# A hybrid decoder block: attention's filling dealt anew with its rows three ahead, and the scan's transposes of y two steps later

## The chip, the cores and the metric

The kernel runs on one core of one Trainium2 chip. The metric is the device time of one launch in microseconds (us). The kernel before takes 2052.62 us, the median of three runs from 2051.77 to 2053.46.

Engine names are those of the profile: PE is the matmul engine (PEld its weight loads), DVE VectorE, ACT ScalarE, POOL GpSimd, SP the engine that issues most DMAs.

## The reference

One layer of a parallel-branch block over 1024 tokens of width 1024, float32:

```python
h = rms_norm(x, norm_w)
proj = h @ w_in
z, xbc, dt_raw, pool_u, pool_gate, qkv, sb_gate, merge = split(proj)
y_ssm  = mamba2_branch(z, xbc, dt_raw, ...) @ w_proj_ssm   # chunked scan, 8 chunks of 128, 32 heads of 64
y_pool = pool_branch(pool_u, pool_gate, ...) @ w_proj_pool
y_sb   = stick_breaking_branch(qkv, sb_gate) @ w_proj_sb   # 16 heads of 64
merged = sum of sigmoid(merge gate) * branch over the three
out = rms_norm(x + merged @ w_out, final_norm_w)

# attention, for a block of 128 queries and all keys before them
z = q k^T * scale
log_beta = log_sigmoid(z); log_one_minus = where(causal, log_sigmoid(-z), 0)
later = reversed exclusive cumsum(log_one_minus)
att = where(causal, exp(log_beta + later), 0);  o = att v

# scan, for a chunk and a head
y = (C B^T * decay) (dt x) + exp(a_cum) C prev_state + d_skip x
state = state * exp(sum a) + B^T (decay_states dt x)
y_ssm_in = rms_norm(y * silu(z)) * ssm_norm_w              # norm over all 2048 channels
```

## The kernel before, in words

A projection product is kept near float32 by splitting both operands in a high and a low part and adding three products, hi x hi, hi x lo, lo x hi (`gemm_b` at L396 with 512 columns, `gemm_a` at L405 with 256). A block of 256 projection columns is 96 such 512-wide matmuls, or 192 of 256 columns. Weights come by DMA as raw halves; ACT rounds the high part (L128) and DVE subtracts it (L129).

The work runs in five parts: norm and convolution inputs, attention, the scan, pooling, and the merge. In attention and in the scan the branch's own work leaves gaps on PE, and blocks of projections that are wanted later are dealt into them as *filling*: a queue of generators, one matmul at a step, from which `fill(ns)` takes as many as a budget in ns allows. A 512-wide matmul counts 216 ns there, a 256-wide one 109. `ensure(name)` runs the queue on until a block is finished.

**Attention** (`attention_part`) goes by units: pair p of heads (8), head hd in the pair (2), and pair ip of query blocks (4, the innermost), 64 units in all. Unit ip holds two *rows*, query blocks 2ip and 2ip+1, whose lengths are 256 ip + 128 and 256 ip + 256 keys.

- `stage_qk` makes one row: PE multiplies q by k into a PSUM tile z (pool of three, L892, L893, L895 for the mask), ACT takes two sigmoids (om L896, be L899), DVE sweeps om with a running product from the right (L901) and multiplies it into be (L902). om has two tiles, be four.
- `stage_tr` transposes a 256 x 256 piece of a unit's two rows on PE (L919) into one of two PSUM tiles; ACT rounds it (L921) and DVE subtracts the rounded part (L922).
- `stage_av` multiplies by v on PE (L945) into one PSUM tile, which ACT copies out at the end of every second unit (L950).

Unit m emits its transposes and, three behind, the products; between these pieces it makes both rows of unit m+1 and deals its share of the filling. The filling belongs to windows of about eight units: blocks ("vz", p+1) and ("qk", p+1) are v, z, q and k of the next pair, and two windows get other blocks of z (`ATT_FILL`). The share of a unit is its weight over the sum of the weights of its window; weights rise with ip from 0.64 to 1.36. PE keeps the order of the code in attention; the other engines are ordered by a scheduler.

**The scan** (`ssd_part`) has 32 steps of (chunk c, head group hg), with PE, DVE, POOL and ACT all in the order of the code. In step m of the loop: loads by SP; `stage_e(m+2)` makes the decay matrix E on ACT (L1149, L1150) and multiplies it with a masked matrix on POOL (L1151); `stage_a(m+1)` transposes x on PE (L1158) and scales it on DVE (L1160 to L1164); `stage_y(m-1)` multiplies y by the gate z on DVE (yz, L1204) and sums squares on ACT (L1205); `finish` makes the root of a whole chunk; `scale(m-5)` multiplies yz by that root on DVE (L1215); half a share of filling; `stage_b(m)` makes y and the state (PE L1174 to L1180, DVE L1183 to L1192, POOL L1186); another half share; `stage_c(m-5)` transposes the scaled yz on PE (ytr, L1221), ACT copies it with a weight (L1224), and SP stores it (L1225). A chunk's four yz lie in one tile, and there are two such tiles. The loop has 32 + 5 turns.

## Time and profile before

| | us |
|---|---|
| median of three runs | 2052.62 |
| profiled execution | 2052.7 |
| its span, first to last instruction | 2050.9 |
| PE busy | 2002.7 (98%) |
| DVE busy | 1392.3 (68%) |
| ACT busy | 955.6 (47%) |
| POOL busy | 301.0 (15%) |

Busy time is a union of an engine's instructions, so PE at 98% has 48 us in which it ran none. The busy time of an operation that two engines contend for includes the time it is held. In the rows, a name left of the arrow is what is written, names right of it what is read.

### The profile page before, as it was taken

The page shows a single profiled execution, that of the slowest core. Times are in us where ns is not written, and L with a number is a line of the kernel's source. Part 1 is how long each engine was busy: PE and PEld are TensorE (multiplying, and loading weights), DVE is VectorE, ACT ScalarE, POOL GpSimd, SP SyncE. Part 2 cuts the span into 40 slices and gives each one's busy share as a digit, 9 for nine tenths or more (in the row PEclk, how much of TensorE's full clock was granted, in tenths as well). Part 3 has the DMA queues.
Part 4 walks back from the last instruction along what each step waited for, and adds up shares of the span by engine and source line. Part 5 has one row for each costly group of instructions (what it writes and reads, how often), then busy time and mean ns, then how long its engine had stood idle before and what let it go on. Part 6 is the DMA issues. An engine that isn't in the chain of part 4 may idle for free.

```text
span 2050.9 us, 28716 instructions
## 1 busy us (share of the span) xinstructions
PE 2002.7 (98%) x10880; PEld 1687.6 (82%) x10880; DVE 1392.3 (68%) x1891; ACT 955.6 (47%) x1936; POOL 301.0 (15%) x412
## 2 busy tenths in 40 slices
PE   8999999999999999999999999999999999999998
PEld 6978888888898898898888987777788788888887
DVE  6786777768377888877788847998857724425434
ACT  4353333323256666656566557666643413313221
POOL 3000000000002211211112114453300002221000
PEclk9999999999999999999999999999999999999999
DMA  5323323233511121121211246665464625443422
GB/s 202 95 97 103 124 82 123 94 113 103 177 46 47 43 68 37 42 75 50 57 38 51 73 160 195 206 204 179 152 210 136 224 92 176 140 137 104 153 73 82
DMA packets 116153, 233.95 MB, mean 114 GB/s; under 512 B 9776, under 2 KB 59696, under 8 KB 116016
## 3 DMA queue, kind: packets, MB, share of 16 engines
q1 hardware_dynamic: 115728, 231.92, 35.2%
q8 instruction: 86, 1.41, 0.3%
q14 instruction: 51, 0.42, 0.1%
q10 hardware_dynamic: 288, 0.20, 0.0%
HBM read 168.38 MB, written 63.70 MB: 113 GB/s over the span
## 4 chain that ended last, share of the span: by engine, by line
PE 66%; DVE 22%; ACT 6%; issue 4%; DMA 1%; DVEq 0%; POOL 0%; SPq 0%; ACTq 0%; POOLq 0%
PE mm L396 17%; PE mmx L396 15%; PE mm L405 10%; PE mmx L299 9%; DVE om L901 4%; PE mmx L405 3%; DVE acc L358 3%; PE av L945 2%; PE mm L299 2%; DVE be L902 2%; PE tr L919 2%; DVE yz L1215 1%; DVE attT L922 1%; DVE w L129 1%; PE yd L1174 1%
## 5 line engine op out<-in xcount | busy, mean ns | idle before, releaser
L396 PE MATMUL mm<-hT,w 128*128 128x512 f32 x1656 | 443.2, 408 | 2.9 <-DVE hT L592 2.8
L396 PEld LDWEIGHTS mm<-hT,w 128*128 128x128 f32 x1656 | 299.3, 189 | 71.7 <-issue 15.3
L405 PE MATMUL mm<-w,hT 128*128 128x256 f32 x2112 | 292.6, 286 | 0.1
L405 PEld LDWEIGHTS mm<-w,hT 128*128 128x128 f32 x2112 | 265.2, 190 | 0.8 <-ACT qb L836 0.5
L396 PE MATMUL mmx<-x,w 128*128 128x512 f32 x1008 | 230.3, 389 | 0.0
L396 PEld LDWEIGHTS mmx<-x,w 128*128 128x128 f32 x1008 | 189.2, 188 | 39.3
L901 DVE TENSOR_TENSOR_SCAN om<-om,zero 128x128 f32<-128x128 f32 (+7 forms) x128 | 181.9, 1422 | 31.9 <-ACT om L896 30.9
L129 DVE TENSOR_TENSOR w<-raw,w 128x1024 fp32r<-128x1024 f32 x104 | 134.0, 1291 | 91.8 <-ACT w L128 91.5
L921 ACT CAST attT<-tr 128x512 fp32r<-128x512 f32 (+2 forms) x224 | 98.7, 441 | 139.4 <-DVE attT L922 89.2
L128 ACT CAST w<-raw 128x1024 fp32r<-128x1024 f32 x104 | 109.1, 1051 | 58.3 <-PE mmx L396 27.7
L922 DVE TENSOR_TENSOR attT<-tr,attT 128x512 fp32r<-128x512 f32 (+2 forms) x224 | 110.4, 495 | 36.7 <-ACT attT L921 35.4
L396 PE MATMUL mm<-x,w 128*128 128x512 f32 x528 | 122.6, 389 | 0.0
L1304 ACT ACTIVATE gt<-gt 128x1024 f32<-128x1024 f32 x32 | 34.0, 1062 | 180.7 <-DMA gt<-d_gate 172.7
L396 PEld LDWEIGHTS mm<-x,w 128*128 128x128 f32 x528 | 99.1, 188 | 20.6
L896 ACT ACTIVATE om<-z 128x128 f32<-128x128 f32 (+2 forms) x192 | 94.2, 502 | 34.9 <-PE z L895 32.9
L902 DVE TENSOR_TENSOR be<-be,om 128x128 f32<-128x128 f32 (+7 forms) x128 | 101.3, 792 | 11.5
L396 PE MATMUL mmx<-hT,w 128*128 128x512 f32 x456 | 105.0, 390 | 0.0
L919 PE MATMUL tr<-cm,be 128*128 128x128 f32 x576 | 91.7, 275 | 8.9 <-DVE attT L922 6.7
L396 PEld LDWEIGHTS mmx<-hT,w 128*128 128x128 f32 x456 | 85.4, 188 | 17.6
L1151 POOL TENSOR_TENSOR E<-E,cbm 128x1024 f32<-128x1024 f32 x32 | 78.5, 2452 | 145.3 <-issue 70.2
L899 ACT ACTIVATE be<-z 128x128 f32<-128x128 f32 (+2 forms) x192 | 93.8, 506 | 0.1
L299 PE MATMUL mmx<-tt,w 128*128 128x512 f32 x360 | 88.5, 397 | 0.3
(258 smaller groups left out, 3507.0 us busy)
## 6 DMA issues: line engine op xcount, KB each, us to landing
raw<-in_wblk SPq DMA_DIRECT2D x148, 512.0 KB, 3.8
E<-d_act SPq DMA_DIRECT2D x32, 512.0 KB, 4.1
gt<-d_gate SPq DMA_DIRECT2D x32, 512.0 KB, 3.8
d_gate<-cx SPq DMA_DIRECT2D x20, 512.0 KB, 5.0
xi<-d_x SPq DMA_DIRECT2D x32, 256.0 KB, 3.1
zs<-d_z SPq DMA_DIRECT2D x32, 256.0 KB, 4.1
d_ssm<-yt SPq DMA_DIRECT2D x32, 256.0 KB, 3.1
xraw<-d_ssm SPq DMA_DIRECT2D x16, 512.0 KB, 5.5
```

The costliest lines, as they stand in the source:

```text
L128: nc.scalar.copy(hi, raw)
L129: nc.vector.tensor_tensor(out=lo, in0=raw, in1=hi.bitcast(F32), op=ALU.subtract)
L299: T.matmul(ps, w[a](i, k), mov[b](j, k), start=first and n == 0, stop=n == 11, skip_group_check=not first)
L396: T.matmul(ps, w(a, k, ct * P, ct * P + P), mov(b, k, half * 512, half * 512 + 512), start=n == 0, stop=n == 23)
L405: T.matmul(ps, sta(a, k, tok * P, tok * P + P), w(b, k, 0, ncol), start=n == 0, stop=n == 23)
L896: A.activation(om[:, c0 : c0 + n], z[:, 0:n], AF.Sigmoid, scale=-0.125)
L899: A.activation(be[:, c0 : c0 + n], z[:, 0:n], AF.Sigmoid, scale=0.125)
L901: V.tensor_tensor_scan(out=rev, data0=rev, data1=self.zero.broadcast_to((P, L)), initial=1.0, op0=ALU.mult, op1=ALU.add)
L902: V.tensor_tensor(out=be[:, 0:L], in0=be[:, 0:L], in1=om[:, 1 : L + 1], op=ALU.mult)
L919: T.transpose(tr[:, c : c + P], b[:, (2 * jc + j) * P : (2 * jc + j + 1) * P], self.ident)
L921: A.copy(at[:, 0, sl], tr[:, sl])
L922: V.tensor_tensor(out=at[:, 1, sl], in0=tr[:, sl], in1=at[:, 0, sl].bitcast(F32), op=ALU.subtract)
```

## The change

In attention, the block ("z", 1) moves from the fifth window's head to the last window, before ("z", 2) and ("z", 3). The tiles of v go from six to five and those of be from four to five. Rows are made from one list, three ahead: three before the loop, then two in each unit, so that unit m makes the second row of unit m+1 and the first row of unit m+2. The weights of the shares are 4.6, 6.1, 8.0 and 1.8 for ip = 0 to 3, and the windows begin one unit earlier.

In the scan, `stage_c` handles step m-7 instead of m-5, `scale` stays at m-5, yz has three tiles, the loop has two more turns, and the filling is shared by 38 instead of 36.

```diff
--- before.py
+++ after.py
@@ -26,8 +26,7 @@
 
 def att_fill():
 
-    order = [[("vz", p + 1), ("qk", p + 1)] for p in range(7)] + [[("z", 2), ("z", 3)]]
-    order[4].insert(0, ("z", 1))
+    order = [[("vz", p + 1), ("qk", p + 1)] for p in range(7)] + [[("z", 1), ("z", 2), ("z", 3)]]
     return order
 
 
@@ -792,8 +791,8 @@
         nc = self.nc
         A, V = nc.scalar, nc.vector
         w = self.block(("vz", p))
-        va = pool.tile([P, 8, P], F32R, tag="v", name=f"va{p}", bufs=6)
-        vb = pool.tile([P, 8, P], F32R, tag="v", name=f"vb{p}", bufs=6)
+        va = pool.tile([P, 8, P], F32R, tag="v", name=f"va{p}", bufs=5)
+        vb = pool.tile([P, 8, P], F32R, tag="v", name=f"vb{p}", bufs=5)
         st[p] = (va, vb)
         for t2 in range(4):
             ps = self.mm().rearrange("p (a b) -> p a b", a=2)
@@ -879,7 +878,7 @@
                 L = (i + 1) * P
                 qh, ql, kst = qk[p][hd], qk[p][2 + hd], qk[p][4 + hd]
                 om = pool.tile([P, S + 4], F32, tag="om", name="om")
-                be = pool.tile([P, S], F32, tag="be", name="be", bufs=4)
+                be = pool.tile([P, S], F32, tag="be", name="be", bufs=5)
                 G.memset(om[:, L : L + 1], 1.0)
                 tq = slice(i * P, i * P + P)
                 zs = []
@@ -954,11 +953,13 @@
                     nc.sync.dma_start(out=self.d_y["sb"][p // 4][rows, p % 4, hs], in_=o[rows])
 
             n = len(units)
-            weight = [0.4 + 0.6 * (u[2] + 1) / 2.5 for u in units]
-            window = [min((m + 1) // 8, 7) for m in range(n)]
+
+            weight = [(4.6, 6.1, 8.0, 1.8)[u[2]] for u in units]
+            window = [min((m + 2) // 8, 7) for m in range(n)]
             share = [weight[m] * len(ATT_FILL[window[m]]) * 96 * 216.0 / sum(x for x, y in zip(weight, window) if y == window[m]) for m in range(n)]
-            for ii in range(2):
-                stage_qk(units[0], ii)
+            rows = [(u, ii) for u in units for ii in range(2)]
+            for _ in range(3):
+                stage_qk(*rows.pop(0))
             late = []
             for m in range(n):
                 u = units[m]
@@ -974,8 +975,8 @@
                 if m == 0:
                     self.fill(share[0] / 2)
                 for q in range(max(len(subs), 2)):
-                    if q < 2 and m + 1 < n:
-                        stage_qk(units[m + 1], q)
+                    if q < 2 and rows:
+                        stage_qk(*rows.pop(0))
                     if q < len(subs):
                         f, v, jc = subs[q]
                         f(v, jc)
@@ -1197,7 +1198,7 @@
             def stage_y(c, hg):
                 y, zs = stt.pop((c, hg)), self.sin_t.pop(("z", c, hg))
                 if hg == 0:
-                    yz = pool.tile([P, 4, 512], F32, tag="yz", name="yz")
+                    yz = pool.tile([P, 4, 512], F32, tag="yz", name="yz", bufs=3)
                     ss = pool.tile([P, 4], F32, tag="ss", name="ss")
                     chunk_yz[c] = (yz, ss)
                 yz, ss = chunk_yz[c]
@@ -1225,7 +1226,7 @@
                 nc.sync.dma_start(out=self.d_y["ssm"][hg][:, :, c * P : c * P + P], in_=yt)
 
             steps = [(c, hg) for c in range(8) for hg in range(4)]
-            share = (len(SCAN_FILL) * 96 * 216.0 - 20000) / 36
+            share = (len(SCAN_FILL) * 96 * 216.0 - 20000) / 38
             n = len(steps)
             self.ssd_open()
             for m in range(3):
@@ -1239,7 +1240,7 @@
             stage_a(*steps[0])
             stage_e(*steps[1])
             self.fill(5000)
-            for m in range(n + 5):
+            for m in range(n + 7):
                 if m + 3 < n:
                     self.ssd_load("a", *steps[m + 3])
                     if steps[m + 3][1] == 0:
@@ -1256,14 +1257,14 @@
                     stage_y(*steps[m - 1])
                     if m % 4 == 0:
                         finish(m // 4 - 1)
-                if m >= 5:
+                if 5 <= m < n + 5:
                     scale(*steps[m - 5])
                 self.fill(share * 0.5)
                 if m < n:
                     stage_b(*steps[m])
                 self.fill(share * 0.5)
-                if m >= 5:
-                    stage_c(*steps[m - 5])
+                if m >= 7:
+                    stage_c(*steps[m - 7])
             while self.step_fill() is not None:
                 pass
         self.dump("ssm0", self.d_y["ssm"][0])
```

DVE in attention, in one of the last heads: the unit ip = 2 in the kernel before, from a subtraction of the filling on. om are the sweeps (written here as SCALAR_TENSOR_TENSOR), be their products, attT the subtractions behind transposes, qla, qlb, ka and kb those of filling, w a weight's.

```order
L830 TENSOR_TENSOR qla_10399<-mm,qa_10397 64x512
L901 SCALAR_TENSOR_TENSOR om<-om,zero 128x896
L922 TENSOR_TENSOR attT<-tr,attT 128x512
L902 TENSOR_TENSOR be<-be,om 128x896
L833 TENSOR_TENSOR qlb_10400<-mm,qb_10398 64x512
L901 SCALAR_TENSOR_TENSOR om<-om,zero 128x1024
L902 TENSOR_TENSOR be<-be,om 128x1024
L922 TENSOR_TENSOR attT<-tr,attT 128x512
L129 TENSOR_TENSOR w_10788<-raw_10395,w_10788 128x1024
L922 TENSOR_TENSOR attT<-tr,attT 128x256
L922 TENSOR_TENSOR attT<-tr,attT 128x128
```

The same unit ip = 2 in the changed kernel, from its first row on:

```order
L900 SCALAR_TENSOR_TENSOR om<-om,zero 128x1024
L901 TENSOR_TENSOR be<-be,om 128x1024
L921 TENSOR_TENSOR attT<-tr,attT 128x512
L900 SCALAR_TENSOR_TENSOR om<-om,zero 128x128
L901 TENSOR_TENSOR be<-be,om 128x128
L921 TENSOR_TENSOR attT<-tr,attT 128x512
L852 TENSOR_TENSOR zsg<-zsg,mm 128x512
L921 TENSOR_TENSOR attT<-tr,attT 128x256
L921 TENSOR_TENSOR attT<-tr,attT 128x128
L852 TENSOR_TENSOR zsg<-zsg,mm 128x512
L951 TENSOR_TENSOR o<-o,oa 64x512
```

Before, the unit's two sweeps are those of 896 and 1024 columns; now they are 1024 and 128, and the sweep of 896 stands in the unit before.

PE in the scan, where the first transposes of y come in (ytr), in the kernel before:

```order
L1174 MATMUL yd<-xdt,E 128x64 x8
L1177 MATMUL yo<-S_11833,bcin 128x512
L1180 MATMUL st<-xw,btok 128x512
L396 MATMUL mm<-hT_110,w_11910 128x512
L396 MATMUL mm<-hT_103,w_11850 128x512 x3
L396 MATMUL mm<-hT_104,w_11850 128x512 x3
L1221 MATMUL ytr<-cm,yz 128x128 x4
L1158 MATMUL xp<-cm,xi 128x128 x4
L396 MATMUL mm<-hT_105,w_11850 128x512 x3
```

And in the changed kernel:

```order
L1175 MATMUL yd<-xdt,E 128x64 x8
L1178 MATMUL yo<-S_11835,bcin 128x512
L1181 MATMUL st<-xw,btok 128x512
L395 MATMUL mm<-hT_110,w_11910 128x512 x3
L395 MATMUL mm<-hT_103,w_12035 128x512 x3
L1222 MATMUL ytr<-cm,yz 128x128 x4
L1159 MATMUL xp<-cm,xi 128x128 x4
L395 MATMUL mm<-hT_104,w_12035 128x512 x3
L395 MATMUL mm<-hT_105,w_12035 128x512 x3
```

The place in the turn is the same, behind the second half share; the first ytr stand two turns later (the state read by yo is that of the fourth head group instead of the second), and the half shares are a little shorter.

## Rows read from the trace of the kernel before

**Rows 1.** Windows: stretch, length, busy us of PE, PEld, DVE, ACT, POOL; clock, DMA.

```profile
553.00:1204.00 651.00, 637.08 (x4430) 573.57 (x4429) 514.84 (x710) 395.92 (x902) 106.06 (x252) 1.00 0.19 53
...
1260.00:1480.00 220.00, 203.14 (x1118) 157.34 (x1117) 194.37 (x259) 148.60 (x411) 96.60 (x55) 0.99 0.60 186
```

**Rows 2.** PE's waits in attention: us, times, longest.

```profile
PE tr L919 <- DVE attT L922: 6.7, 11, 1.2
PE av L945 <- ACT oa L950: 2.8, 5, 1.1
PE tr L919 <- DVE be L902: 2.1, 6, 0.9
```

**Rows 3.** Windows inside attention, columns as above.

```profile
880.00:960.00 80.00, 80.00 (x587) 74.21 (x586) 55.93 (x79) 43.91 (x99) 8.67 (x26) 1.00 0.21 61
960.00:1204.00 244.00, 235.34 (x1690) 212.90 (x1689) 197.76 (x268) 147.85 (x337) 41.29 (x97) 1.00 0.18 53
```

**Rows 4.** Timeline of PE: start, us, line, op; idle before and its releaser.

```profile
1122.00 0.66 PE L919 MATMUL tr<-cm,be 128*128 128x128 f32 x4 [1.24 <-DVE attT L922]
```

**Rows 5.** Timeline of DVE at the same place.

```profile
1117.44 2.29 DVE L901 TENSOR_TENSOR_SCAN om<-om,zero 128x1024 f32<-128x1024 f32 x1
...
1121.25 0.69 DVE L922 TENSOR_TENSOR attT<-tr,attT 128x512 fp32r<-128x512 f32 x1
```

**Rows 6.** PE's waits in the scan.

```profile
PE ytr L1221 <- DVE yz L1215: 14.8, 16, 2.0
```

**Rows 7.** Timeline of PE, transposes of y in the scan.

```profile
1266.63 0.60 PE L1221 MATMUL ytr<-cm,yz 128*128 128x128 f32 x4
...
1342.55 0.63 PE L1221 MATMUL ytr<-cm,yz 128*128 128x128 f32 x4 [0.60 <-DVE yz L1215]
...
1351.26 0.63 PE L1221 MATMUL ytr<-cm,yz 128*128 128x128 f32 x4 [1.12 <-DVE yz L1215]
...
1469.98 0.63 PE L1221 MATMUL ytr<-cm,yz 128*128 128x128 f32 x4 [1.43 <-DVE yz L1215]
```

**Rows 8.** Timeline of ACT in the same interval.

```profile
1343.22 1.14 ACT L1224 ACTIVATE yt<-ytr,cols 128x128 f32<-128x128 f32 x4 [1.18 <-PE ytr L1221]
1344.23 2.45 ACT L1149 ACTIVATE E<-E,dt_all 128x128 f32<-128x128 f32 x8
```

**Rows 9.** Timeline of POOL in the same interval.

```profile
1347.90 2.93 POOL L1151 TENSOR_TENSOR E<-E,cbm 128x1024 f32<-128x1024 f32 x1 [4.59 <-PE yo L1177]
```

**Rows 10.** Timeline of DVE in the same interval.

```profile
1348.50 2.62 DVE L1215 TENSOR_SCALAR yz<-yz,r 128x512 f32<-128x512 f32 x1
```

**Rows 11.** DVE's groups in the scan: busy us, mean ns, idle before.

```profile
L1215 DVE TENSOR_SCALAR yz<-yz,r 128x512 f32<-128x512 f32 x32 | 39.6, 1245 | 0.0
```

**Rows 12.** Line L1215 alone: ns min/median/max.

```profile
L1215 DVE TENSOR_SCALAR yz<-yz,r x32: 476/484/2668, 1264.0 to 1489.1; 128x512 f32<-128x512 f32 x32
```

**Rows 13.** DVE's groups in attention: busy us, mean ns, idle before.

```profile
L901 DVE TENSOR_TENSOR_SCAN om<-om,zero 128x128 f32<-128x128 f32 (+7 forms) x128 | 181.9, 1422 | 31.9 <-ACT om L896 30.9
L922 DVE TENSOR_TENSOR attT<-tr,attT 128x512 fp32r<-128x512 f32 (+2 forms) x224 | 110.4, 495 | 36.7 <-ACT attT L921 35.4
L902 DVE TENSOR_TENSOR be<-be,om 128x128 f32<-128x128 f32 (+7 forms) x128 | 101.3, 792 | 11.5
```

**Rows 14.** Timeline of PE in attention, an undisturbed piece.

```profile
1074.01 0.40 PE L892 MATMUL z<-ka,qa 128*128 128x512 f32 x1
...
1075.08 0.63 PE L945 MATMUL av<-attT,va 128*128 128x256 f32 x4
...
1075.55 1.24 PE L405 MATMUL mm<-w,hT 128*128 128x256 f32 x9
...
1076.62 0.60 PE L919 MATMUL tr<-cm,be 128*128 128x128 f32 x4
...
1076.98 1.19 PE L405 MATMUL mm<-w,hT 128*128 128x256 f32 x8
```

**Rows 15.** Timeline of DVE in the scan, addition of xk.

```profile
1333.34 2.50 DVE L1187 TENSOR_TENSOR y<-y,xk 128x512 f32<-128x512 f32 x1
```

## The prediction

> **What bounds the kernel now.** I read the busy times of stretches first, then who TensorE waited for, then the order of time at the places of the longest waits. TensorE (PE) is the engine to look at: in attention it works 637.1 of 651 us, in the scan's steady part 203.1 of 220 [rows 1]. Its matmuls stay the same in number and shape, so what can be won there is its idle time: 13.9 us and 16.9 us. The reader should see that VectorE (DVE), at 514.8 and 194.4 us, is not the fuller engine in either stretch, yet ends most of PE's waits.
>
> In attention the waits end mostly with DVE's subtraction that frees a transpose's PSUM tile [rows 2]. PE emits 64 units there, by 16 head passes of four (ip = 0 to 3), with projection matmuls dealt between them. Where a third block is dealt into the window, from 880 to 960 us, PE does not idle at all, while the 244 us behind it hold 8.7 us of idle time [rows 3]. One wait shows the mechanism: at 1122.00 the first transposes of a unit ip = 3 had waited 1.24 us [rows 4], and DVE had a 1024-column scan running from 1117.44 and came to the subtraction only at 1121.25 [rows 5]. The two longest rows are swept in the unit before, and DVE is late by its end.
>
> In the scan all of PE's listed waits of size are the transposes of y waiting for their scaling, 14.8 us in 16 waits [rows 6]. From the first to the last of 25 such groups in the steady part there are 24 steps in 203.4 us, 8.47 us each [rows 7]; 220 us are 26 steps, so a step is 7.81 us of PE, 7.48 of DVE and 0.65 of PE idle. Two of the groups stand 8.71 us apart, and that interval is a loop through four engines: transposes at 1342.55, ScalarE's copy at 1343.22, its next decay work E at 1344.23 [rows 8], GpSimd's product on that E at 1347.90 [rows 9], VectorE's scaling, begun at 1348.50 and 2.62 us long [rows 10], next transposes at 1351.26. The mean scaling takes 1.25 us [rows 11], the median 0.48 [rows 12]: it is stretched when GpSimd's 2.93 us product runs, and in this interval the loop brings the two together again.
>
> **The change part by part.**
>
> *Attention, rows three ahead.* A unit makes the second row of the next unit and the first of the one after, instead of both rows of the next. By DVE's totals over 73,728 columns (16 passes of 4608) a row costs (181.9 + 101.3)/73,728 = 3.84 ns a column and a subtraction 110.4/73,728 = 1.50 ns [rows 13]. For PE a row of 1024 columns takes 1.07 us (1074.01 to 1075.08), and transposes and products of 512 columns 0.36 + 0.47 us: 1.04 and 1.62 ns a column. Nine filling matmuls take 1.07 us [rows 14], 119 ns each where the code counts 109, so I take filling at 1.09 times its count. The rest of DVE's 514.8 us, 121 us, goes over 17 blocks x 20.7 x 1.09 = 384 us of filling: 0.32 us for each us.
> Before, units make 896, 1408, 1920, 384 columns and get 3.3, 4.6, 5.8, 7.05 us of filling by the code's count. PE: 5.2, 7.9, 10.6, 11.2 us; DVE: 5.2, 8.3, 11.5, 6.8. DVE falls behind by 0.4 + 0.9 = 1.3 us up to the unit ip = 3 and then has 4.4 us to spare.
> After, they make 1152, 1664, 1152, 640 columns and get 4.65, 6.2, 8.1, 1.8 us. PE: 6.9, 9.9, 12.3, 5.8; DVE: 6.6, 9.9, 9.3, 6.0. DVE is never more than some 0.2 us behind, so the wait that I showed goes. What is late next is the unit ip = 3 itself: with so little filling, PE comes to a next transpose every 1.3 us (0.36 + 0.47 + a quarter of 1.98), with two PSUM tiles in turn, while DVE has 6.0/4 = 1.5 us of work for each. Queued behind a waiting transpose are this unit's products and the next rows, and DVE's sweeps wait for these. I take 0.45 us a pass, 7 us in all, where it is 13.9/16 = 0.87 now; the bounds are 1 us in all (never late) and 16 x 1.24 = 20 us (each pass waits as long as at 1122.00). That saves 6.9 us, between 12.9 and -5.9.
>
> *Attention, z block 1 moved to the end; one buffer from v to be.* Filling moves from a window without idle time to the last one, whose units had the least: total PE work is equal, and the window that lost it becomes like the others. It is in the 0.45. Its loads and stores move in SP's queue with it; the scan reads this block's output for its third step at the earliest, and block 3 was already as late. With five v tiles a new one takes over the tile of the last pair's first head, whose products were emitted some units earlier: I cost it at nothing, at worst one wait like the 1.24 us in each of 7 pairs, 9 us, which only the high end holds.
>
> *Scan, transposes two steps behind.* PE no longer asks for a scaling of the same step; the third tile of yz keeps the earlier data readable. The loop above is cut. Each of 32 steps gets 152 ns less filling (96 x 216 x 6 - 20,000 shared by 38 instead of 36), 4.9 us that PE does after the last step, where it has no other work to wait for: this costs nothing as long as PE is the bound. PE's step is then 7.81 - 0.15 = 7.66 us. DVE's is 7.48 with the stretched scalings in it and 6.7 without them (1.25 - 0.48 less). Two engines that near to each other still wait for each other at times (weight splits and root terms fall into some steps only), so I do not take zero: 0.25 us a step, 6.5 us over 26, against 16.9. That saves 10.4 us. The bounds: 15.9 us, if 1 us of idle time is left, and a loss of 4.9 us, if the step stays at 8.47. The stores of the copies stand two steps later in SP's queue, with the loads of those steps in front; their data are ready by then, so loads no longer wait behind an unfinished copy.
>
> One row speaks against this part: GpSimd's product runs from 1347.90 to 1350.83 and the scaling beside it ends 0.3 us behind [rows 9, 10], and the addition of xk, with both inputs in SBUF, once took 2.50 us [rows 15]. The Trainium skill ("GPSIMD Engine Reference", Key points) says that GpSimd shares its SBUF interfaces with VectorE and contends with instructions in a two-port mode or with two SBUF inputs. The trace agrees, with these two rows; by that rule the stretch may only move from the scaling to a neighbour, which is the first rival below.
>
> *Sum.* The profiled execution took 2052.7 us, span 2050.9 and 1.8 around it, which is the runs' median of 2052.62. 2052.7 - 6.9 - 10.4 = 2035.4.
>
> **The rivals.**
> 1. *VectorE stays the bound of the scan.* GpSimd's product meets y times z or the addition of xk instead of the scaling, a step stays at 8.47 us, and PE waits at the y products' PSUM tile instead. For it: the 2.50 us addition [rows 15]. Against it: GpSimd's start was tied to PE's late transposes, and it comes earlier without them. Attention's 6.9 stand, the 4.9 us of filling now add to the end: 2052.7 - 6.9 + 4.9 = 2050.7. Chance 0.15.
> 2. *The thin unit, slower.* In units ip = 3 PE meets both waits that the trace knows, 1.24 us for a transpose and 1.1 for the product's PSUM tile [rows 2, 4], in each of 16 passes: 37 us of idle time instead of 13.9. With the scan's gain: 2052.7 + 23.5 - 10.4 = 2065.8. It decides above (13.9 + 10.4)/16 = 1.5 us a pass. For it: DVE 6.0 against PE 5.8 us there. Against it: DVE comes in without arrears, out of a unit with 3 us to spare. Chance 0.1.
> 3. *Both idle times go nearly to nothing* (1 us left in each): 2052.7 - 12.9 - 15.9 = 2023.9. For it: PE does not idle at all in the window with more filling [rows 3]. Against it: that window had half as much again. Chance 0.13.
> 4. *It does not do what it says*: the row order on DVE decides the waits, not the filling, and attention stays at 13.9 while the scan gains a part, 4 us: 2048.7. Chance 0.04.
>
> **How the numbers follow.** The forecast, 2035.4, has 0.58; its own range is 2027 to 2046, from attention's 3 to 12 and the scan's 3 to 10 us of idle time. The range that is to hold 8 of 10 reaches to the first and fourth rival and half-way to the third: 2026 to 2052. A measurement of this kernel can tell 0.2%, about 4 us, from no change. Faster by more: the forecast, rival 3, and a part of 4, 0.75. Within: rival 1 nearly whole and a part of 4, 0.14. Slower: rival 2 and a little of rival 1, 0.11.
>
> **What would show it.** Right: between the attention's start and end PE's idle time near 7 us and no wait over 1 us in front of units ip = 3; in the scan no wait of the transposes for the scaling, groups of them 7.9 us apart, GpSimd's product ending nearer to the start of the scaling than 2.4 us. Wrong: waits of 0.7 us or more in most units ip = 3; the y products waiting for DVE's addition in most steps; groups still over 8.3 us apart; new waits where the pooling part starts.

## The result and the profile after

The changed kernel takes 2067.95 us (median of four runs, 2067.40 to 2070.05), the one before 2052.49 beside it (four runs, 2051.77 to 2053.46): 1.0077 times as long, 95% interval 1.0065 to 1.0089. The forecast was 2035.4, with 2026 to 2052 around it: wrong in sign, and outside its range.

The profiled execution's span grew from 2050.9 to 2066.0 us. Where the 15.1 us arose is read at two marks on PE: the long run of filling that opens the scan's part begins at 1215.45 instead of 1204.04 (its first matmul), and the last transposes of y at 1511.72 instead of 1496.80. So attention lost 11.4 us and the scan another 3.5; from there to the end nothing changed (554.1 us before, 554.3 after).

**Attention.** PE's waits in the changed kernel from 553 to 1204 us (us, times, longest):

```profile
PE tr L918 <- DVE attT L921: 22.4, 30, 1.5
PE av L944 <- ACT oa L949: 1.1, 3, 0.4
```

The same windows as in [rows 1], of the changed kernel, the second one set 11.3 us later:

```profile
553.00:1204.00 651.00, 627.48 (x4347) 563.42 (x4347) 518.77 (x701) 392.37 (x891) 106.79 (x250) 1.00 0.18 52
1271.30:1491.30 220.00, 207.18 (x1097) 159.04 (x1096) 197.39 (x263) 145.13 (x402) 96.30 (x54) 0.95 0.60 186
```

Against [rows 1 and 2], PE's idle time in attention rose from 13.9 to 23.5 us, nearly all of it at the transposes. The scan is the strange line: PE idles *less* there, 12.8 us instead of 16.9, and the time grew. The column to see is the clock: 0.95 instead of 0.99.

One unit ip = 3 shows attention's wait. PE, from the unit's first transposes to its last (start, us, tile; idle before and releaser):

```profile
1085.74 0.60 PE L918 MATMUL tr<-cm,be 128*128 128x128 f32 x4
...
1088.64 0.66 PE L918 MATMUL tr<-cm,be 128*128 128x128 f32 x4 [1.37 <-DVE attT L921]
...
1091.64 0.55 PE L918 MATMUL tr<-cm,be 128*128 128x128 f32 x3 [1.41 <-DVE attT L921]
```

DVE in the same stretch:

```profile
1085.34 0.69 DVE L951 TENSOR_TENSOR o<-o,oa 64x512 f32<-64x512 f32 x1 [0.85 <-ACT o L950]
1085.94 0.68 DVE L900 TENSOR_TENSOR_SCAN om<-om,zero 128x256 f32<-128x256 f32 x1
1086.76 1.23 DVE L901 TENSOR_TENSOR be<-be,om 128x256 f32<-128x256 f32 x1
1087.91 0.68 DVE L921 TENSOR_TENSOR attT<-tr,attT 128x512 fp32r<-128x512 f32 x1
1088.51 0.94 DVE L900 TENSOR_TENSOR_SCAN om<-om,zero 128x384 f32<-128x384 f32 x1
```

And POOL:

```profile
1086.10 1.60 POOL L952 TENSOR_TENSOR o<-o,gt 64x512 f32<-64x512 f32 x1 [3.63 <-DVE o L951]
```

The first subtraction (1087.91) stands behind a sweep and its product, and these behind the addition of two copies of the output o, which waits 0.85 us for ACT. The product be, of only 256 columns, takes 1.23 us, where the sixteen of this size take 0.42 in the mean in the kernel before: POOL multiplies o by its gate just then. The unit's matmuls are few, so nothing covers the chain, and the next but one transposes wait for its PSUM tile.

This unit is not alone. To attention's end the transposes wait 23.2 us in 31 times, and 20.8 of these us stand before the third and fourth transposes of units ip = 3; the other 2.4 stand before the third transposes of units ip = 2.

**The scan.** PE's waits in the changed kernel from 1204 to 1500 us:

```profile
PE yd L1175 <- DVE y L1185: 7.8, 6, 2.9
PE yd L1175 <- DMA zs<-d_z: 3.0, 2, 1.8
PE yd L1175 <- DMA xi<-d_x: 1.2, 1, 1.2
```

The 16 waits of [rows 6], the longest of 2.0 us, are gone, and the transposes of y wait for nothing. In their place stand waits of the y products, nine in these rows and a few of them long. Three of the nine are put down to loads (zs, xi), but they too end with DVE's addition, as at 1320.09:

```profile
1319.14 0.69 DVE L1185 TENSOR_TENSOR y<-y,yd 128x512 f32<-128x512 f32 x1
1320.09 3.08 PE L1175 MATMUL yd<-xdt,E 128*128 128x64 f32 x16 [1.83 <-DMA zs<-d_z]
```

The addition ends at 1319.83 and PE starts 0.26 us later; at 1354.78 and 1466.04, the other two, it is the same 0.25 or 0.26 us. PE at the longest wait:

```profile
1360.77 1.62 PE L395 MATMUL mm<-hT,w 128*128 128x512 f32 x6
1365.28 3.65 PE L1175 MATMUL yd<-xdt,E 128*128 128x64 f32 x16 [2.89 <-DVE y L1185]
1368.72 2.02 PE L1178 MATMUL yo<-S,bcin 128*128 128x512 f32 x2
```

Sixteen y products take 1.89 us at a granted clock of 1.00 (at 1310.92 in the same trace) and 3.65 here. Windows around it, columns as above:

```profile
1364.00:1368.00 4.00, 2.72 (x13) 2.75 (x14) 3.93 (x7) 2.86 (x8) 0.98 (x1) 0.64 0.99 287
1368.00:1372.00 4.00, 4.00 (x10) 2.18 (x9) 3.18 (x6) 0.72 (x2) 2.24 (x3) 0.51 0.54 153
```

Behind the wait PE is busy all the time, at a granted clock of 0.51, which is the lower of its two levels (1.2 instead of 2.4 GHz). Such stretches look full in a table of busy time. I take the time lost in them as the sum of (1 - clock) x 4 us over 78 windows of 4 us, from 1200 to 1512 in the kernel before and from 1212 to 1524 in the changed one, where the scan begins 11.4 us later: 10.2 us after, 1.7 before. PE's idle time in the same windows is 12.8 us after, 16.9 before. The two together: 23.0 against 18.6, 4.4 us more, beside the 3.5 that the marks give.

What PE waits for at 1365.28 is seen on DVE:

```profile
1357.56 2.70 DVE L1205 TENSOR_TENSOR yz<-y,zs 128x512 f32<-128x512 f32 x1
1360.19 1.26 DVE L1216 TENSOR_SCALAR yz<-yz,r 128x512 f32<-128x512 f32 x1
1362.48 1.23 DVE L128 TENSOR_TENSOR w<-raw,w 128x1024 fp32r<-128x1024 f32 x1 [1.02 <-ACT w L127]
1363.62 0.68 DVE L1184 TENSOR_TENSOR y<-yo,dt_all 128x512 f32<-128x512 f32 x1
1364.34 0.69 DVE L1185 TENSOR_TENSOR y<-y,yd 128x512 f32<-128x512 f32 x1
```

The addition that frees the one yd tile (1364.34) is late by a chain: the product with z is held (2.70 instead of 0.68 us), ACT squares it and only then rounds the weight, DVE waits 1.02 us for that rounding, and both additions stand behind. Before, PE was tied to the same turn's scaling; now it runs up to this tile and stops once. In the mean a step is no shorter: 21 groups of transposes of y, from 1292.53 to 1462.18, stand 8.48 us apart, where 8.47 was read before, but unevenly: 12.8 and 13.5 us across the two longest waits and mostly 7.1 to 8.8 elsewhere.

### The profile page after: what moved, and what is told of

It reads as the page before. It is cut to its first block, busy times and chain, and to the rows that moved or that the text cites. A ratio compares the mean times of both kernels' runs of the same rounds, so it can differ in the third digit from the quotient of the medians.

```text
span 2066.0 us, 28678 instructions
## 1 busy us (share of the span) xinstructions
PE 2011.4 (97%) x10880; PEld 1692.2 (82%) x10880; DVE 1405.8 (68%) x1891; ACT 956.4 (46%) x1936; POOL 302.5 (15%) x412
## 4 chain that ended last, share of the span: by engine, by line
PE 64%; DVE 24%; ACT 6%; issue 4%; DMA 1%; DVEq 0%; POOL 0%; SPq 0%; ACTq 0%; POOLq 0%
PE mm L395 15%; PE mmx L395 14%; PE mm L404 10%; PE mmx L298 9%; DVE om L900 4%; PE mmx L404 3%; DVE acc L357 3%; DVE be L901 2%; PE mm L298 2%; DVE attT L921 2%; PE av L944 2%; PE yd L1175 2%; PE tr L918 2%; ACT E L1150 1%; PE z L891 1%
## 5 line engine op out<-in xcount | busy, mean ns | idle before, releaser
L901 DVE TENSOR_TENSOR be<-be,om 128x128 f32<-128x128 f32 (+7 forms) x128 | 106.8, 835 | 12.1
L918 PE MATMUL tr<-cm,be 128*128 128x128 f32 x576 | 91.0, 276 | 23.2 <-DVE attT L921 23.2
L918 PEld LDWEIGHTS tr<-cm,be 128*128 128x128 f32 x576 | 66.3, 140 | 39.5 <-DVE attT L921 31.5
```

The lines of the kernel that those rows point to most:

```text
L901: V.tensor_tensor(out=be[:, 0:L], in0=be[:, 0:L], in1=om[:, 1 : L + 1], op=ALU.mult)
L918: T.transpose(tr[:, c : c + P], b[:, (2 * jc + j) * P : (2 * jc + j + 1) * P], self.ident)
```

## The experiments

Times are medians; "ratio" is to the kernel before on the same chip (2052.2 to 2053.1 there), with its 95% interval. Runs were made on several chips, so two kernels are compared by their differences to the kernel before beside each. Theory A at the start: attention loses in the units with little filling, and in the scan the hold only moves on.

**One part at a time.** att_only has the changed attention and the scan of before, scan_only the reverse.

> Attention's part of the change alone; the scan is as it was before. Theory A (units ip = 3 have too little filling, so that transposes wait for VectorE there): PE's waits for attT stay near 23 us, attention ends about 11 us later than before, 2063.5 us in all. Rival B (the change in the scan is what costs, by a later step): near 2053. Rival C (attention's loss comes from something that the two parts do together): between the two, near 2057.

> The scan's part of the change alone; attention is as it was before. Theory A (VectorE stays the bound of the scan, its held operations move from the scaling to the product with z and the addition of xk, and TensorE's clock falls after the longer waits): 2056 us, 3 to 4 us slower, no waits of the transposes, several of yd for the addition. Rival (the scan would have gained by itself and loses only because it is entered otherwise from attention): 2042 to 2048.

att_only took 2063.54 us, ratio 1.0051 [1.0036, 1.0066]; scan_only 2056.78, 1.0016 [1.0006, 1.0025]. Beside the kernel before, 10.4 and 3.7 us are lost: the two add up to 14.1 of the 15.5 us, and A held in both. All ten executions of scan_only had a mean granted clock of 0.992 to 0.994, the twenty of the kernel before beside them 0.996 or 0.997; a clock lower by 0.003 over 2052 us would be some 6 us.

**GpSimd's product left out.** before_noE and scan_noE are the scan of before and the changed one without this line:

```diff
-                G.tensor_tensor(out=E, in0=E, in1=cbm[...]..., op=ALU.mult)
```

> The kernel before with GpSimd's product of E and the masked matrix (L1151) left out, so that the decay matrix goes unmasked into the y products and y is not the reference's. Theory A (the scan is bound by VectorE's operations that are held while this product runs): held time of yz, its scaling and the addition of xk falls from 40 us to about 12 (GpSimd's product for the state remains), PE's waits for the scaling fall from 14.8 to under 5 us, time 2040 to 2046. Rival (PE waits for the order of the loop, not for held operations): waits over 10 us, time over 2049.

> The scan's part of the change alone, with the same product left out (y is not the reference's). Theory A: no waits of yd for VectorE over 3 us in all, no falls of the clock, time 2037 to 2043, a little below the kernel before without the product. Rival 1 (loads set the scan's pace now): waits of yd for DMA stay, time over 2050. Rival 2 (transposes two steps later are worth nothing even without held operations): same as the kernel before without the product.

2031.10 us, ratio 0.9899 [0.9885, 0.9914], and 2031.89, 0.9903 [0.9888, 0.9918]. Both came out under A's ranges (2040 to 2046, 2037 to 2043); in the second it is rival 2 that held. PE does not wait in either scan. DVE's three operations beside the product are, in the kernel before, the scaling of [rows 11] and these two (busy us, mean ns, idle before):

```profile
L1187 DVE TENSOR_TENSOR y<-y,xk 128x512 f32<-128x512 f32 x28 | 29.0, 1036 | 1.0
L1204 DVE TENSOR_TENSOR yz<-y,zs 128x512 f32<-128x512 f32 x32 | 28.1, 879 | 0.1
```

in scan_only:

```profile
L1204 DVE TENSOR_TENSOR yz<-y,zs 128x512 f32<-128x512 f32 x32 | 38.8, 1212 | 0.1
L1187 DVE TENSOR_TENSOR y<-y,xk 128x512 f32<-128x512 f32 x28 | 31.2, 1114 | 1.0
L1215 DVE TENSOR_SCALAR yz<-yz,r 128x512 f32<-128x512 f32 x32 | 30.9, 969 | 0.4 <-POOL r L545 0.4
```

and in scan_noE:

```profile
L1203 DVE TENSOR_TENSOR yz<-y,zs 128x512 f32<-128x512 f32 x32 | 21.8, 680 | 0.1
L1186 DVE TENSOR_TENSOR y<-y,xk 128x512 f32<-128x512 f32 x28 | 19.4, 692 | 1.0
L1214 DVE TENSOR_SCALAR yz<-yz,r 128x512 f32<-128x512 f32 x32 | 15.9, 504 | 0.4 <-POOL r L545 0.4
```

100.9 us with POOL's product, 57.1 without: 44 us are held. Before, the three took 28.1, 29.0 and 39.6 us, 96.7, so 40 were held. The change took 8.7 us from the scaling and put 12.9 on its neighbours. Without the product the edit is worth nothing (0.8 us apart). With it, the kernel before is 21 us slower and scan_only 24. Leaving the product out takes away two things at once, the hold on DVE and the time that E waits for POOL; no run parts them. The Trainium skill ("GPSIMD Engine Reference", Key points) names both kinds of victim, instructions in a two-port mode and those with two SBUF inputs. The traces agree as to the two operations with both inputs in SBUF, the product with z and the addition of xk. The scaling is held too; that it runs in a two-port mode no run here shows. The product xk, which reads one input from PSUM, kept its 0.68 us at 1314.54 in the changed kernel, while POOL's product ran from 1314.39.

**The scaling on ACT** (scan_act, from scan_only):

```diff
-                V.tensor_scalar(yz[:, hg], yz[:, hg], r, None, op0=ALU.mult)
+                A.activation(yz[:, hg], yz[:, hg], AF.Copy, scale=r)
```

> The scan's part of the change alone, but the scaling of yz is done by ScalarE (activation Copy with the root as scale) instead of VectorE. VectorE loses 0.48 us a step unheld, and one of its three operations that can be held. Theory A (VectorE is the bound): the step falls by 0.4 to 0.6 us, time 2044 to 2050. Rival (held time only moves on again): product with z and addition of xk are held for the same 44 us, time 2053 to 2057.

2053.54 us, ratio 1.001 [1.0001, 1.0019]: the time is the rival's. Beside the kernel before it loses 1.4 us where scan_only loses 3.7, and the two intervals overlap, so a gain is not shown. The rival's 44 us of held time did not stay: DVE's other two took 37.5 and 28.2 us, 24.5 more than in scan_noE.

**Weights of the filling**, with the rows three ahead and the scan of before: att_oldw has those of before, att_bal and att_mid lie between, att_more gives the unit ip = 3 most.

```diff
-            weight = [(4.6, 6.1, 8.0, 1.8)[u[2]] for u in units]
+            weight = [0.4 + 0.6 * (u[2] + 1) / 2.5 for u in units]   # att_oldw
+            weight = [(4.4, 5.8, 6.3, 4.0)[u[2]] for u in units]     # att_bal
+            weight = [(3.8, 5.2, 6.0, 5.5)[u[2]] for u in units]     # att_mid
+            weight = [(2.6, 3.9, 5.0, 9.0)[u[2]] for u in units]     # att_more
```

> Rows three ahead, z block 1 at the end and five v tiles as in the changed attention, but shares of filling by the weights of before (0.64, 0.88, 1.12, 1.36); the scan is as it was before. Theory A (the thin share is the cause): the waits for attT fall from 23 us to 5 to 12, time 2046 to 2054. Rival (the order of the rows on VectorE is the cause, whatever the shares): waits stay over 18 us, time over 2059.

> As the changed attention, but the weights 4.4, 5.8, 6.3, 4.0 instead of 4.6, 6.1, 8.0, 1.8, so that a unit ip = 3 gets about 4 us of filling, taken from ip = 2; the scan is as it was before. Theory A: about 2 us more per unit ip = 3 take away most of its 1.5 us of waiting, attention idle 5 to 9 us, time 2045 to 2049. Rival (the row order is the cause): 2060.

> Changed attention alone, with weights 2.6, 3.9, 5.0, 9.0: units ip = 3 get 9 us of filling. With 1.8 it took 2063.5, with 4.0 2060.5, with the old weights (7.0 on this scale) 2049.2. Theory A (a unit ip = 3 wants filling while VectorE and ScalarE take its four transposes): little waiting in ip = 3, 2046 to 2050, unless units ip = 0 to 2 run short. Rival (the best lies at VectorE's sum of work, between 1.8 and 7): over 2052.

> Changed attention alone with weights 3.8, 5.2, 6.0, 5.5, between those that took 2060.5 and the old ones (3.3, 4.6, 5.8, 7.0 on this scale) that took 2049.2. Theory A (one best share between): 2048 to 2056. Rival (the old weights are good for another reason, where pieces of filling end against the rows, and single times jump): under 2046 or over 2058.

att_oldw 2049.20 us, ratio 0.998 [0.9971, 0.9989]; att_bal 2060.50, 1.0037 [1.0023, 1.0051]; att_mid 2060.53, 1.0035 [1.0022, 1.0048]; att_more 2075.47, 1.0114 [1.0098, 1.0131]. The waits of the transposes were 11.6, 13.4, 14.4 and 27.2 us in 12, 24, 12 and 15 times. So the old weights are the best of the five, and between att_only and att_oldw, which differ by the weights alone, lie 14.3 us. Theory A held in att_oldw and in none of the other three: it missed att_bal by 12 us, where the rival had named 2060, and att_mid and att_more came out in the rivals' ranges too. A's picture of one thin unit was too small. In att_mid nearly all of the transposes' waits (14.2 of 14.4 us) stand in a second place, before the third transposes of units ip = 2; in att_bal 6.0 us stand there and 6.5 in units ip = 3. One of them in att_mid, on DVE:

```profile
995.36 3.19 DVE L900 TENSOR_TENSOR_SCAN om<-om,zero 128x1024 f32<-128x1024 f32 x1
998.68 1.23 DVE L901 TENSOR_TENSOR be<-be,om 128x1024 f32<-128x1024 f32 x1
999.83 0.68 DVE L921 TENSOR_TENSOR attT<-tr,attT 128x512 fp32r<-128x512 f32 x1
```

and PE:

```profile
1000.57 0.55 PE L918 MATMUL tr<-cm,be 128*128 128x128 f32 x3 [1.77 <-DVE attT L921]
```

With rows three ahead the longest sweep stands ahead of this unit's first subtraction, so it too wants filling; what one unit gets the other loses. That is read from the trace; no run isolates it. It doesn't say why the old weights are the best: with them no unit ip = 3 waits, but a unit ip = 2 gets no more filling than in att_mid (5.8 against 6.0), and all 11.6 us of its waits stand there. Nor is att_oldw's gain of 3.9 us to be seen in idle time: its profiled span is 4.2 us shorter than that of the kernel before, and PE's idle time from 552 to 1200 us only 1.3 (12.6 against 13.9).

**Rows two ahead, the new weights alone** (att_two, from the kernel before):

> The kernel before (rows two ahead, six v tiles, z block 1 in the fifth window, scan unchanged) with only the new weights 4.6, 6.1, 8.0, 1.8. By sums of work a unit, VectorE is under PE in every unit (5.6 of 6.6, 8.9 of 9.6, 12.3 of 13.1, 5.0 of 5.5 us). Theory A (a thin unit ip = 3 makes waits by the order inside the unit, whatever the sums): waits for attT over 15 us, 2058 to 2066. Rival (sums decide, and the rows three ahead put too much on units ip = 3): 2043 to 2050.

```diff
-            weight = [0.4 + 0.6 * (u[2] + 1) / 2.5 for u in units]
+            weight = [(4.6, 6.1, 8.0, 1.8)[u[2]] for u in units]
```

2065.03 us, ratio 1.0058 [1.0043, 1.0073]: the thin share loses without any change of rows, in the time that A gave. The waits for attT came to 13.9 us, under A's 15; another 6.8 stand before filling that waits for ACT's copies of q.

**Three smaller parts of attention**, each from att_only: att_odve makes the product of o and its gate on DVE, att_z1 puts ("z", 1) back, att_tr3 has three PSUM tiles for transposes and two for rows.

```diff
-                G.tensor_tensor(out=o[rows], in0=o[rows], in1=gt[rows], op=ALU.mult)
+                V.tensor_tensor(out=o[rows], in0=o[rows], in1=gt[rows], op=ALU.mult)   # att_odve
...
+    order[4].insert(0, ("z", 1))                                  # att_z1
...
-            pz = self.ps(ctx, "a_z", 3); ptr = self.ps(ctx, "a_tr", 2)
+            pz = self.ps(ctx, "a_z", 2); ptr = self.ps(ctx, "a_tr", 3)   # att_tr3
```

> Changed attention alone, with the gate's product (o times gt, L952, 1.6 us on GpSimd) moved to VectorE. In the traced unit ip = 3 this product ran beside VectorE's be of 256 columns, which took 1.23 us instead of 0.42, right in front of the subtraction that the third transposes waited for. Theory A (part of the thin unit's waits is this held operation): waits for attT fall from 23 to about 15 us, time 2055 to 2059 against 2063.5. Rival (ScalarE's copies and the sweeps in front of the subtraction make the wait by themselves): waits stay over 20 us, time 2062 or more.

> Changed attention alone, with z block 1 back at the head of the fifth window. Theory A (a thin unit waits wherever it is): two passes win about 1.5 us each, the last window loses as much, 2061 to 2066. Rival (the block's place makes the loss, since a window of 8 units lost 20 us of filling): 2052 to 2056.

> Changed attention alone, with three PSUM tiles for the transposes and two instead of three for the rows. Theory A (third and fourth transposes of a thin unit wait for a tile that the first and second still hold): waits for attT fall from 23 to under 8 us; some waits of the rows for ScalarE come in, 2050 to 2056. Rival (PE only moves the wait on to the products, which want the same subtractions): waits of av for attT take its place, over 2059.

2060.14 us, ratio 1.0039 [1.0025, 1.0053]; 2061.28, 1.0044 [1.003, 1.0058]; 2063.52, 1.0048 [1.0033, 1.0063]. Beside the kernel before, 7.8, 8.9 and 10.6 us are lost, where att_only loses 10.4. The first two differences, 2.6 us for the held product of be (between what the theories said) and 1.5 for the place of the block (A's range), lie inside the intervals, so neither is shown. The hold itself is: in att_odve the be of 256 and of 1024 columns take 0.42 and 1.22 us in the mean, in att_only 0.68 and 1.58, 10 us of DVE's time in all, while the gate's product takes 22 us there. In att_tr3 PE's waits in attention read:

```profile
PE z L891 <- ACT be L898: 19.4, 21, 1.5
PE tr L918 <- DVE attT L921: 1.6, 4, 0.5
```

The ring of two was what the transposes waited for, but its tile came from the rows, and they wait now; the time is the same. PE's idle time from 552 to 1200 us fell from att_only's 23.5 to 21.0, but 6.8 us went to the clock there, where att_only lost none. The rival had the time but not the place of the waits.

**GpSimd's product on DVE, one step later.** scan_edve is the kernel before with this, best1 is att_oldw with it, best2 is best1 with the transposes two steps later, best3 is best2 with three quarters of a step's filling ahead of the y products.

```diff
-                G.tensor_tensor(out=E, in0=E, in1=cbm[...]..., op=ALU.mult)   # in stage_e(m + 2)
+                V.tensor_tensor(out=E, in0=E, in1=cbm[...]..., op=ALU.mult)   # behind stage_a(m + 1)
```

> Rows three ahead with the old weights and z block 1 at the end, the scan with its transposes as before, and the product of E with the masked matrix moved from GpSimd to VectorE, one step later (between the scaling of x and the product with z). VectorE's step has no held time but that of the state's product: 7.48 - 1.25 + 1.2 = 7.4 us, under PE's 7.8. Theory A: 2049.2 less 10 to 18 us, 2031 to 2039. Rival (VectorE with 1.2 us more a step becomes the bound by its fixed order): over 2049.

> The kernel before with only the product of E moved from GpSimd to VectorE one step later (attention and transposes of y as before). Theory A (of the 17 us that the run with old weights and this product gained, 13 to 14 are this product's): 2037 to 2041. Rival (the gain needs the attention as well): over 2045.

> The same with the transposes of y two steps later, as in the change. Theory A (without held operations the two steps are worth little): within 3 us of the run before it. Rival (with VectorE fuller, late scalings hold PE, and two steps of slack pay): 4 us or more faster than it.

best1 took 2035.18 us, ratio 0.9918 [0.9905, 0.9932]: 17 us under the kernel before, 33 under the changed one. scan_edve took 2041.40, 0.9942 [0.9925, 0.9958], so some 11.5 us are the product's move, less than A's 13 to 14. best2 took 2042.88, 0.9955 [0.9942, 0.9967], on best1's chip; neither theory had expected the edit to *cost* 7.7 us where hardly anything is held. By the windows of 4 us, best1 idles 6.9 us and loses nothing to the clock, best2 idles 8.3 and loses 5.1. Three windows of best2 from 1340 us on, behind the start of a wait of 2.79 us:

```profile
1340.00:1344.00 4.00, 1.21 (x7) 0.76 (x5) 3.07 (x4) 4.00 (x13) 0.00 (x0) 0.89 0.85 287
1344.00:1348.00 4.00, 4.00 (x17) 3.48 (x17) 4.00 (x7) 1.24 (x2) 0.00 (x0) 0.50 0.51 157
1348.00:1352.00 4.00, 4.00 (x14) 2.41 (x13) 3.11 (x8) 0.72 (x2) 1.73 (x2) 0.76 0.64 199
```

**More filling ahead of the y products** (scan_split from scan_only, best3 from best2), to cover the long waits:

```diff
-                self.fill(share * 0.5)
+                self.fill(share * 0.75)
                 if m < n:
                     stage_b(*steps[m])
-                self.fill(share * 0.5)
+                self.fill(share * 0.25)
```

> The scan's change alone (transposes two steps later), with three quarters of a step's filling ahead of the y products and one quarter behind them instead of half and half; attention as before. Theory A (the few long waits of the y products for VectorE's addition, and the lower granted clock in the 4 to 8 us behind each, are what the change costs in the scan: 5.2 us more lost by the clock than before): with some three filling matmuls (0.6 us at full clock) more ahead of each y product the longest waits fall from 2.9 to about 2 us, the clock falls less often, and the time comes down from 2056.8 to 2046 to 2053. Rival B (VectorE's step, with the held operations in it, sets the pace, and PE's waits only move): the waits turn up at the state product or at the transposes of x, as much in sum, and the time stays at 2055 to 2059.

> The version with rows three ahead and the old weights, GpSimd's product on VectorE and the transposes two steps later (2042.9), with three quarters of the filling ahead of the y products. Theory A: without held operations VectorE has slack in each step, so more filling ahead of the y products covers its latency: waits of the y products fall from 7.4 us to under 3, no stretch with a low clock, 2032 to 2038, as the version with the transposes left where they were (2035.2) or better. Rival B: the long waits come from ScalarE's and VectorE's order (weight roundings in the queue ahead of the y additions), which more filling ahead brings along too: 2040 to 2045.

2060.49 us, ratio 1.0037 [1.0023, 1.0051], and 2046.53, 0.9969 [0.9959, 0.998]: beside the kernel before 3.7 and 2.9 us slower than their parents. Theory A missed both, and both lie above B's ranges as well. The intervals of scan_only and scan_split just touch, those of best2 and best3 overlap. best3's longest wait grew to 3.05 us on PE,

```profile
1312.64 1.73 PE L1178 MATMUL yd<-xdt,E 128*128 128x64 f32 x7 [3.05 <-issue]
```

for which the profile names no releaser; PE starts 0.1 us behind the end of DVE's second addition, and DVE is behind a weight's rounding again, though nothing was held for over 1 us:

```profile
1309.99 1.23 DVE L128 TENSOR_TENSOR w<-raw,w 128x1024 fp32r<-128x1024 f32 x1 [1.81 <-ACT w L127]
1311.13 0.68 DVE L1187 TENSOR_TENSOR y<-yo,dt_all 128x512 f32<-128x512 f32 x1
1311.85 0.69 DVE L1188 TENSOR_TENSOR y<-y,yd 128x512 f32<-128x512 f32 x1
```

More filling did not cover the wait. What is dealt ahead of the products can bring the weight's split with it, and on DVE that stands ahead of the additions, as B had it; this is read from the one place. Idle time and clock in the 78 windows can be set beside the profiled spans, from parent to child. scan_split keeps 15.5 us of idle time and loses 11.9 us to the clock instead of 6.9 (5.0 more; its span grew by 4.2). best3 idles 2.1 and loses 3.4 us more (5.5; span 3.5). From before to scan_only it is -1.3 and 5.2 us (3.8; span 4.1), from best1 to best2 1.4 and 5.1 (6.5; span 9.7). In three of the four pairs the clock's share is about as large as the growth of the span, in the fourth about half of it.

## Why the prediction was wrong

- *Attention, "DVE is never more than some 0.2 us behind", and "I take 0.45 us a pass".* This step failed. The four units' sums were right as sums and said nothing about the order within a unit: in the thin one DVE's addition of o, a sweep and a held product stand ahead of the first subtraction. Idle time came to 23.5/16 = 1.5 us a pass, just at the point from which rival 2 decides, and over the upper bound of 20 us. Measured 10.4 us lost (att_only) where 6.9 were to be saved. That is rival 2's unit (chance 0.1), at less than half its size: it had waits of 1.24 and 1.1 us in every pass, 23.5 us more, and the trace has waits of 0.2 to 1.5 us before the third and fourth transposes. The prediction knew the doubtful unit (DVE 6.0 against PE 5.8 us) and still let the sums decide.
- *Attention, the filling's weights as the means.* att_oldw shows the opposite: the rest of attention's change (rows three ahead, windows a unit earlier, five tiles of be and v, z block 1 at the end) gains 3.9 us as long as the old weights stay. att_two shows that the new weights lose 12 us without that rest.
- *Attention, z block 1 "in the 0.45".* It was 1.5 us by itself (att_z1), which is not clear of noise.
- *Scan, "The loop above is cut" and DVE's step of 6.7 us.* The transposes' wait went, as said. The stretch of the scaling did not: held time went from 40 to 44 us, since GpSimd's product met the product with z and the addition of xk. This step failed too. It is rival 1's mechanism (chance 0.15), with its step of 8.47 us (8.48 measured), and what the row that spoke against the step had shown; only the y products did not wait in most steps, but in nine. Measured 3.7 us lost (scan_only) where 10.4 were to be saved.
- *Scan, the price of a wait.* The sum counted idle time only. PE's idle time did fall, though by 1.3 us and not by 10.4, and behind fewer, longer waits stood stretches at the lower clock, 5.2 us more. No term and no rival held that. In the kernel before the clock fell once in the scan's trace (1.7 us), in att_only's trace of the same scan not at all.
- *The rivals as alternatives.* Rival 2 was worked out with the scan's gain in it, rival 1 with attention's. Both came true in part, and no case had both; by their own numbers that would be 2052.7 + 23.5 + 4.9 = 2081, further out than the 2067.95 measured. That rival 2's 2065.8 lies close to the measured time is luck: its attention is 13 us too slow and its scan 14 us too fast.

What stays open: which of rows-ahead, the windows, the order of z and the tiles makes att_oldw's 3.9 us, and why weights between the old and the new lose; how the 21 us of POOL's product divide between the hold on DVE and the wait for E; and whether the clock's falls in the scan are caused by the length of a wait alone, since no run lengthened a single wait and left the rest.

## What to carry to other kernels

When one engine's operation holds up another's, moving the victim in time may only pick another victim, as here, where the reordering lost 3.7 us. Try taking one of the two operations to the other engine (here 11.5 us gained); what it costs at most shows when it is left out (21 us). A removed wait may have been a brake that kept an engine close to its producers: ask where it will stop next, for how long at once, and what the clock does behind that. A balance of sums over a unit was not enough here, with rings of two tiles; walk through the in-order queue of the engine that frees the tile, in the unit with the least cover.

## What the runs showed of the hardware

- POOL's product of 128x1024 takes 2.3 to 2.9 us, and beside it DVE operations of 0.48 to 0.69 us take up to 2.8 us; the same product takes 1.21 us on DVE, and moving it there made the kernel faster (scan_edve) although DVE's queue is the one that PE waits for.
- After the scan's longest waits, of 1.8 to 3.05 us, windows of 4 us show PE busy nearly all the time at a granted clock of 0.5 to 0.8, mostly 0.5 to 0.6, for one or two windows in a row (changed kernel, scan_only, best2, best3). Shorter waits can stand ahead of such a stretch too: in the changed kernel a window at 0.64 follows a wait of 1.2 us (1466.04), and in att_tr3 windows at 0.54 to 0.86 follow pairs of waits of 1.0 to 1.5 us. In the scan of before, with 16 waits of up to 2.0 us and 1.4 us more idle time than scan_only, one such stretch occurred.
